# Another weight sequence for a list-scheduled attention block

## The chip, the cores and the metric

The kernel runs on one core of a Trainium2 chip. The metric is device time in microseconds for one call, the median of three runs. Five engines work side by side and meet through semaphores: TensorE (PE) multiplies, with its weight loads (PEld) recorded apart; VectorE (DVE), ScalarE (ACT) and GpSimd (POOL) work on tiles; SyncE (SP) mostly issues transfers.

## The reference

One residual layer of an encoder, S = 512 tokens, D = 1024, all in float32. A single input projection feeds two token mixers. A is multi-head latent attention: low-rank latents are normalised and projected up to 8 heads, with a rotary key that all heads share. B is sparse attention: a light indexer scores the keys, each query keeps 256 of them, with a relative bias. Each branch is gated, projected and weighted, the sum goes through an output projection and a last norm.

```python
h = rmsnorm(x, norm_g)
cq, ckv, kr, za, qb, kb, vb, zb, qi, ki, wi, ga, gb = split(h @ w_in)
# A: q = rms(cq) @ w_uq, [k_nope, v] = rms(ckv) @ w_ukv, rope on q_pe and kr
logits = q_nope . k_nope + q_pe . k_pe            # chunk-causal mask, softmax, @ v
# B: score = sum_h relu(qi_h . ki) * wi_h ; idx = top_k(score, 256)
logits = qb . kb[idx] * scale + rel_bias[bucket]  # softmax, @ vb[idx]
y = sigmoid(ga)*((A*silu(za)) @ w_o_a) + sigmoid(gb)*((B*silu(zb)) @ w_o_b)
out = rmsnorm(x + y @ w_out, final_g)
```

(shortened; splits, biases and reshapes are left out)

## The kernel before, in words

Every float32 operand is split into a high part and a remainder in a rounded format, and each product is made of three TensorE matmuls: high by high, high by low, low by high (`mm3`, which calls `mm`). Tokens stand in four tiles of 128, the 1024 input channels in eight. x is loaded and normalised, turned, and multiplied by the latent and indexer columns first. Then the weights are gone through tile by tile, each 128 x 1024 or less.

What sets the order of all work is a scheduler that runs while the kernel is built, the class `Flow`. Each piece of work is a thread, a generator that yields steps (an instruction group, with the engines that could do it and a duration), requests for a buffer, or conditions. `Flow.run` holds a clock for each engine and one for the transfers, asks for each waiting step when it could start (`start`: engine free, inputs written, readers of the output done), adds to that a safety time for PE and SP (`settled`, 1 to 2 us behind another engine's result), and emits the step with the lowest key. What it emits is fixed: at run time each engine works its list in order and waits at semaphores.

The weight tiles go through three threads, in the order of a list of jobs. `fetcher` has SP load each tile into one of four raw buffers, `splitter` splits it (a cast on ACT, the remainder on DVE or POOL), `multiplier` runs the job's matmuls. The string `QUEUE` gives the jobs' sequence by two-letter names: ga and gb are gate tiles, za and zb tiles of the SiLU paths, pe the rotary part of q, ma0 to ma3 two heads each of the up-projection of A, va its values, sb q and k of B, and ou the output projection's loads; names in capitals are pairs of tiles that `seven` multiplies with seven products in place of eight.

Eight PSUM banks ps0 to ps7 carry all products. A step that writes a bank waits for the readers of what stood in it. Around the change these names matter: `latraw`, the raw latents, scaled by rstd and by sm and then turned by PE (`turn`) into ps banks, from which ACT and DVE make `lat` with two instructions; L932 (L928 after), the relative bias as a product of a one-hot tile, copied by ACT; L883 (L879 after), one head's indexer scores for one token tile, then a ReLU on ACT in the bank, then a multiply-add into `mask` on DVE; and `mla_job`, where ACT and DVE split a head pair into `th` and `op`, SP moves halves of them to other partitions and adds the rotary rows (`qpe`, `kpeh`, `kpel`), and L1582 to L1584 (L1570 to L1572 after) form the logits. Four loads, jobs 7 to 10 of the list, are held back by `hold` until SP has issued 2 or 6 further transfers (`PASSED`), and one remainder of B's values is emitted late, at the next `add` of `seven` (`passed_by`).

Of the kernel before, what the change touches and what calls it, by code (L numbers as in the profile page):

```python
# [43 lines left out]
class Buf:  # L44


    def __init__(self, tile, name):
        self.tile, self.name, self.w, self.r, self.written = tile, name, 0.0, 0.0, False
        self.by, self.reads = None, {}
# [90 lines left out]
class Flow:  # L140
# [57 lines left out]
    def run(self, stop=None):  # L198
        while self.threads:
# [64 lines left out]
DRAW = 53  # L264
# [6 lines left out]
def tile_block(ctx: ExitStack, tc: tile.TileContext, a: dict, out: bass.AP, bias_dram: bass.AP):  # L271
# [25 lines left out]
    ps_bufs = set(id(b) for b in PS.free)  # L297

# [113 lines left out]

    def mm(ps, pairs, start, stop, more=False):
# [6 lines left out]
        t = len(pairs) * (0.0133 + pairs[0][1].n / 2400)  # L420
# [9 lines left out]
    def turn(parts):  # L430
# [6 lines left out]
        return pe(0.107 * len(parts), [d for d, _ in parts], [s for _, s in parts] + [ident.all], emit, len(parts))  # L437

    held = []

    def hold(n, emit):

        return lambda: held.append([n, emit])

    def passed():
        for x in list(held):
            x[0] -= 1
            if not x[0]:
                held.remove(x)
                x[1]()  # L450

    def dma(dst, src):

        d, s = (v.ap if isinstance(v, View) else v for v in (dst, src))
        n = 4
        for x in (dst.ap if isinstance(dst, View) else src.ap).shape:
            n *= x
        return Step([("SP", n / 360000.0, lambda: (nc.sync.dma_start(d, s), passed()))], bufs(dst), bufs(src))
# [25 lines left out]
    def pool_dma_out(dst, src):  # L484
        step = Step([("POOL", 1.03, lambda: nc.gpsimd.dma_start(dst, src.ap))], [], bufs(src))
# [391 lines left out]
    def scores(i):  # L877
        n = P * (i + 1)
        work = mask[i]  # L879
        for h in range(NH):  # L880
            yield Until(lambda: h in qs and ks)
            ps = yield bank("lg")
            yield pe(0.005 + n / 2400, [ps.all], [qs[h].all, ks[0].all], lambda: nc.tensor.matmul(  # L883
# [265 lines left out]
    def values2():  # L1149
# [69 lines left out]
        def take(half, out):  # L1219
            v = yield Get(VV)  # L1220
            for u in range(2):
# [4 lines left out]
                step = lo_part(lo, src, hi)  # L1226
                if half == 1 and u == 0:

                    step.options = [(e, t, lambda emit=emit: passed_by.append(emit)) for e, t, emit in step.options]
                yield step  # L1230
# [141 lines left out]
    qpe, operands = {}, {}  # L1372
# [34 lines left out]
    def mla_job(j):  # L1407
        lat_users[0] += 1

        def take(ps, kind):  # L1410
# [31 lines left out]
            if j == 3 and not kind:  # L1442
                put(*qpe[0], *qpe[1])
# [110 lines left out]
    def mla_head(h):  # L1554
# [18 lines left out]
        for i in ORDER:  # L1573
# [12 lines left out]
            yield pe(3 * (0.0133 + nn / 2400), [ps.all], [qh.all, ql.all, kh.all, kl.all], emit, 3)  # L1586
# [497 lines left out]
SUMS_AT = ("a", 5)  # L2084
# [83 lines left out]
```

## Time and profile before

| what | value |
|---|---|
| time, median of 3 runs | 423.46 us (423.2 to 423.58) |
| span of the profiled execution | 421.2 us |
| PE busy | 413.7 us (98%), 2314 matmuls |
| DVE, ACT, POOL busy | 372.8, 265.6, 125.2 us |
| mean granted TensorE clock | 0.995 |
| share of PE in the chain of waits | 96% |
| HBM read, written | 50.49 MB, 4.21 MB |

The span runs from the first to the last instruction of one profiled execution; the timed runs are 2.26 us longer, at the median. In rows of the timeline the first number is the start in us, the second the time that the group took; `x6` counts its instructions, and a bracket tells how long the engine stood idle before it and for whom. PE rows overlap, since matmuls are pipelined: the distance from one start to the next is what a matmul costs. Buffer numbers are left out there: `ps` is any bank.

### The profile page before, as it was taken

The numbers are of one execution on the slowest core, as the hardware profiler recorded it, in microseconds if no ns is written. First come the engines' busy times: TensorE is split into PE (matmuls) and PEld (weight loads), VectorE is DVE, ScalarE is ACT, GpSimd is POOL, SyncE is SP. The second block draws the span as 40 slices with busy tenths as digits, with TensorE's granted clock in tenths as the row PEclk, the third lists the DMA queues.
The fourth block names the chain that finished last, engine by engine and source line by source line (L and its number), as shares of the span: only waits on it lengthen the run. The fifth ranks groups of instructions, "written<-read, shape, count | busy, mean of one in ns | idle before, by whom it ended". The sixth has DMA issues, their size and how long they took to land.

```text
span 421.2 us, 7078 instructions
## 1 busy us (share of the span) xinstructions
PE 413.7 (98%) x2314; PEld 364.3 (86%) x2314; DVE 372.8 (89%) x797; ACT 265.6 (63%) x596; POOL 125.2 (30%) x139
## 2 busy tenths in 40 slices
PE   8999999999999999999999999999999999999994
PEld 7999878888888888888999988998998888888883
DVE  4879889569999999999999999979799768999995
ACT  5877778586754748625578677694597444336624
POOL 0047768543464669400012000200100000120652
PEclk9999999999999999999999999999999999999998
DMA  7992135665266441444652347144542887248305
GB/s 258 382 337 77 48 94 191 172 206 127 75 156 184 89 151 51 119 146 149 151 163 75 110 142 188 56 166 129 153 138 68 292 296 242 102 148 305 123 1 199
DMA packets 30645, 65.89 MB, mean 156 GB/s; under 512 B 4776, under 2 KB 6200, under 8 KB 30608
## 3 DMA queue, kind: packets, MB, share of 16 engines
q1 hardware_dynamic: 28256, 61.66, 47.4%
q10 hardware_dynamic: 1584, 2.62, 1.7%
q0 software_dynamic: 768, 1.15, 0.9%
q8 instruction: 18, 0.29, 0.3%
q14 instruction: 19, 0.16, 0.1%
HBM read 50.49 MB, written 4.21 MB: 130 GB/s over the span
## 4 chain that ended last, share of the span: by engine, by line
PE 96%; DVE 1%; DMA 1%; issue 0%; POOL 0%; ACT 0%; POOLq 0%; SPq 0%; ACTq 0%
PE ps L418 86%; PE ps L435 5%; PE ps L1583 1%; PE ps L1584 1%; PE ps L1582 1%; PE ps L883 1%; DMA normg<-norm_g 1%; DVE s_xr L357 1%; POOL sm L396 0%; DVE s_rg L357 0%; DVE s_rg L376 0%; ACT s_rg L329 0%; POOLq L2164 0%; ACT s_xg L329 0%; PE ps L932 0%
## 5 line engine op out<-in xcount | busy, mean ns | idle before, releaser
L418 PE MATMUL ps<-s_h,s_w 128*128 128x512 f32 (+1 forms) x732 | 169.9, 379 | 0.0
L418 PEld LDWEIGHTS ps<-s_h,s_w 128*128 128x128 f32 x732 | 128.3, 189 | 22.0
L320 ACT CAST s_w<-raw 128x512 fp32r<-128x512 f32 (+3 forms) x124 | 71.8, 593 | 18.8 <-DMA raw<-w_o 9.3
L348 POOL TENSOR_TENSOR s_w<-raw,s_w 128x512 fp32r<-128x512 f32 (+2 forms) x39 | 48.5, 1255 | 48.1 <-ACT s_w L320 44.2
L346 DVE TENSOR_TENSOR s_w<-raw,s_w 128x512 fp32r<-128x512 f32 (+2 forms) x85 | 55.7, 668 | 4.7 <-ACT s_w L320 3.7
L418 PE MATMUL ps<-s_ys,s_w 128*128 128x512 f32 x192 | 43.8, 389 | 0.0
L418 PEld LDWEIGHTS ps<-s_ys,s_w 128*128 128x128 f32 x192 | 36.0, 188 | 7.5
L329 ACT ACTIVATE s_p<-s_p,sm 128x128 f32<-128x128 f32 (+3 forms) x62 | 32.7, 550 | 5.0 <-DVE sm L1662 4.3
L418 PE MATMUL ps<-s_wo,s_mg 128*128 128x512 f32 (+1 forms) x156 | 33.2, 373 | 0.0
L418 PE MATMUL ps<-s_w,s_xg 128*128 128x328 f32 (+1 forms) x192 | 32.5, 323 | 0.0
L418 PEld LDWEIGHTS ps<-s_wo,s_mg 128*128 128x128 f32 x156 | 27.6, 188 | 5.2
L418 PEld LDWEIGHTS ps<-s_w,s_xg 128*128 128x128 f32 x192 | 31.4, 188 | 0.0
L346 DVE TENSOR_TENSOR s_ph<-ps,s_ph 128x384 fp32r<-128x384 f32 (+1 forms) x48 | 27.6, 593 | 1.0 <-ACT s_ph L320 0.7
L320 ACT CAST s_ph<-ps 128x384 fp32r<-128x384 f32 (+1 forms) x48 | 23.4, 515 | 6.4 <-PE ps L435 5.0
L329 ACT ACTIVATE s_p<-ps,sm 128x128 f32<-128x128 f32 (+3 forms) x32 | 16.8, 527 | 15.7 <-DVE sm L1565 15.6
L348 POOL TENSOR_TENSOR s_p<-s_bias,mask 128x128 f32<-128x128 f32 (+2 forms) x5 | 4.2, 854 | 74.0 <-DMA s_bias<-bias_scratch 39.6
L905 DVE MAX8 sm<-mask 128x8 f32<-128x384 f32 (+2 forms) x48 | 25.7, 549 | 0.2
L906 DVE MATCH_REPLACE8 mask<-sm,mask 128x384 f32<-128x384 f32 (+2 forms) x48 | 25.9, 541 | 0.0
L418 PE MATMUL ps<-s_ph,vv 128*128 128x512 f32 (+3 forms) x128 | 25.1, 318 | 0.0
L435 PE MATMUL ps<-ident,s_p 128*128 128x128 f32 x160 | 23.1, 273 | 0.0
L418 PEld LDWEIGHTS ps<-s_ph,vv 128*128 128x128 f32 x128 | 21.0, 188 | 2.4
L348 POOL TENSOR_TENSOR s_wo<-raw,s_wo 128x512 fp32r<-128x512 f32 x3 | 13.2, 4420 | 28.3 <-ACT s_wo L320 28.3
(194 smaller groups left out, 769.6 us busy)
## 6 DMA issues: line engine op xcount, KB each, us to landing
raw<-w_out SPq DMA_DIRECT2D x18, 512.0 KB, 3.3
s_op<-s_op SPq DMA_DIRECT2D x36, 128.0 KB, 2.3
raw<-w_ga SPq DMA_DIRECT2D x8, 512.0 KB
raw<-w_gb SPq DMA_DIRECT2D x8, 512.0 KB
raw<-w_o SPq DMA_DIRECT2D x16, 256.0 KB, 4.2
s_xn<-x SPq DMA_DIRECT2D x8, 256.0 KB, 4.8
bias_scratch<-s_sig ACTq DMA_DIRECT2D x8, 256.0 KB, 3.0
raw<-w_za SPq DMA_DIRECT2D x4, 512.0 KB, 4.7
```

The costliest lines, as they stand in the source:

```text
L320: nc.scalar.copy(dst.ap, src.ap)
L329: nc.scalar.activation(dst.ap, src.ap, func, **kw)
L346: opts.append(("DVE", 0.07 + 0.00104 * x.n, lambda: nc.vector.tensor_tensor(dst.ap, x.ap, y.ap, op=op)))
L348: opts.append(("POOL", 0.15 + 0.0021 * x.n, lambda: nc.gpsimd.tensor_tensor(dst.ap, x.ap, y.ap, op=op)))
L357: lambda: nc.vector.scalar_tensor_tensor(dst.ap, x.ap, sc(s), y.ap, op0=op0, op1=op1))],
L418: nc.tensor.matmul(ps.ap, l.ap, r.ap, start=start and i == 0, stop=stop and i == len(pairs) - 1, skip_group_check=more)
L435: nc.tensor.transpose(d.ap, s.ap, ident.tile)
L883: yield pe(0.005 + n / 2400, [ps.all], [qs[h].all, ks[0].all], lambda: nc.tensor.matmul(ps.tile[:, :n], qs[h].tile[:96, TOK[i]], ks[0].til ...
L905: yield Step([("DVE", t, lambda: nc.vector.max(m8.tile, work.tile))], [m8], [work])
L906: yield Step([("DVE", t, lambda: nc.vector.match_replace(work.tile, m8.tile, work.tile, MARK))], [work], [m8])
L1582: nc.tensor.matmul(o, q0[0:100], k0[0:100], start=True, stop=False)
L1583: nc.tensor.matmul(o, q0[0:96], k1[0:96], start=False, stop=False)
```

## The change

The scheduler's model gets other clocks. A step that reads a PSUM bank now also waits, in the model, for other engines' reads of it. A transfer takes SP 0.46 or 0.55 us to issue (0.05 before, beside a queue clock of its own), its first packet comes 1.0 or 1.2 us later, its duration is scaled by 0.935 (1.8 from buffer to buffer), and it lands 1.4 us behind that. A matmul counts at least 0.1155 us, a transpose 0.109. The seed of the threads' random nudges is another. The string QUEUE is another sequence. The held loads (`PASSED`, `hold`, `passed`) and the late remainder (`passed_by`) are gone, and the four tiles of rotary queries are given back once all four head pairs have used them, in whatever order, no more at pair 3.

```diff
@@ Flow.start
+            if b.bank:
+                for e, r in b.reads.items():
+                    if e != eng:
+                        s = max(s, r + self.lat(e, eng))
@@ Flow.run
-                self.free["SP"] = s + 0.05
-                self.hw = max(self.hw, s) + (0.65 if step.ins and step.outs else 0.475)
-                self.dma = max(self.dma, self.hw + 0.65)
-
-                self.dma += dur * (SLOW if self.dma < 7.3 else 1.0)
-                end = self.dma + (2.2 if step.ins and step.outs else 1.0) + step.late
+                both = step.ins and step.outs
+                self.free["SP"] = s + (0.55 if both else 0.46)
+                first = s + (1.2 if both else 1.0)
+                self.dma = max(self.dma, first) + dur * (1.8 if both else 0.935) * (SLOW if self.dma < 7.3 else 1.0)
+                end = max(self.dma, first + dur * (1.8 if both else 1.47)) + LANDING + step.late
...
-DRAW = 53
+DRAW = 46
...
+    def span(columns):
+
+        return max(0.0133 + columns / 2400, 0.1155)
...
-        t = len(pairs) * (0.0133 + pairs[0][1].n / 2400)
+        t = len(pairs) * span(pairs[0][1].n)
...
-        return Step([("SP", n / 360000.0, lambda: (nc.sync.dma_start(d, s), passed()))], bufs(dst), bufs(src))
+        return Step([("SP", n / 360000.0, lambda: nc.sync.dma_start(d, s))], bufs(dst), bufs(src))
...
-            if n in PASSED:
-
-                step.options = [("SP", step.options[0][1], hold(PASSED[n], step.options[0][2]))]
             yield step
...
-            step = tt(dst, part(ps), y, ALU.add)
-            return step.then(lambda: [passed_by.pop()() for _ in list(passed_by)])
+            return tt(dst, part(ps), y, ALU.add)
...
-            if j == 3 and not kind:
-                put(*qpe[0], *qpe[1])
+            if not kind:
+                qpe_users.append(j)
+                if len(qpe_users) == 4:
+                    put(*qpe[0], *qpe[1])
...
-QUEUE = 'ga0 ga1 pe ma0 va0 ga2 za0 ma1 va1 ga3 za1 ma2 ga4 za2 ma3 ga5 za3 sb0 zb0 ga6 ga7 sb1 VB GB0 GB1 sb2 zb1 GB2 GB3 sb3 zb2 GB4 GB5 ou zb3 gb6 ou gb7 ou'
+QUEUE = 'ga0 va0 ga4 ga7 za0 pe ga1 ma0 ma2 ga2 za2 ma1 gb3 va1 ma3 zb0 sb1 sb0 zb1 ga5 ga6 za1 VB za3 ou sb2 sb3 gb7 ga3 GB0 GB1 zb3 ou GB2 GB6 GB4 GB5 ou zb2'
+LANDING = 1.4
-PASSED = {7: 2, 8: 2, 9: 2, 10: 6}
```

What this does to the lists shows at two places. The first is PE's list at the relative bias and the second set of latents, some 300 rows in. Before, one one-hot product (into ps4, later one into ps3) stands apart, with other matmuls behind it:

```order
L932 MATMUL ps4_96<-s61_oh109_599,rbs_126 8x320
L883 MATMUL ps7_99<-s30_qs139_740,s21_qs102_570 128x256
L883 MATMUL ps5_97<-s30_qs139_740,s21_qs102_570 128x384
L418 MATMUL ps1_93<-s27_h121_653,s72_w130_704 128x512
...
L435 MATMUL ps6_98<-ident_100,s5_latraw132_717 128x128
...
L932 MATMUL ps3_95<-s71_oh129_694,rbs_126 8x320
L435 MATMUL ps4_96<-ident_100,s5_latraw132_717 128x128
...
L418 MATMUL ps0_92<-s25_h111_607,s18_w140_745 128x512
...
L435 MATMUL ps3_95<-ident_100,s5_latraw132_717 128x128
```

After, both products follow each other, and scores take their banks eight transposes later; ps4 is turned into twice (four rows each, one shown):

```order
L879 MATMUL ps7_99<-s16_qs137_733,s61_qs110_592 128x256
L879 MATMUL ps3_95<-s16_qs137_733,s61_qs110_592 128x384
L928 MATMUL ps5_97<-s7_oh121_652,rbs_126 8x320
L928 MATMUL ps0_92<-s34_oh127_697,rbs_126 8x320
L444 MATMUL ps4_96<-ident_100,s71_latraw130_711 128x128
...
L444 MATMUL ps1_93<-ident_100,s71_latraw130_711 128x128
...
L879 MATMUL ps5_97<-s16_qs137_733,s61_qs110_592 128x512
L879 MATMUL ps0_92<-s16_qs137_733,s18_qs126_687 128x256
L427 MATMUL ps6_98<-s37_h128_703,s3_w133_719 128x512
...
L444 MATMUL ps4_96<-ident_100,s71_latraw130_711 128x128
...
L427 MATMUL ps7_99<-s21_w139_737,s0_lat135_727 128x256
```

The work between a product and the next use of its bank has become less. ACT's list of the new kernel, which serves these banks, has there:

```order
L334 ACTIVATE s2_latraw132_717<-ps3_95,rstd_124 128x384
L334 ACTIVATE junk_113,sm3_79<-ps4_96,rstd_124 128x384
L334 ACTIVATE s17_latraw138_735<-ps4_96,rstd_124 128x384
...
L325 CAST s37_h128_703<-s10_tmp122_658 128x512
L325 CAST s21_w139_737<-raw0_66 128x512
L334 ACTIVATE ps7_99<-ps7_99 128x256
L334 ACTIVATE ps3_95<-ps3_95 128x384
L325 COPY s22_tmp142_748<-ps5_97 8x320
L325 COPY s23_tmp143_749<-ps0_92 8x320
L334 ACTIVATE s32_lat149_815<-ps4_96,glat_102 128x512
```

The four scalings into `latraw` are new on ACT; they were DVE's before.

The second place is SP's list where the operands of the second pair of heads are moved. Before (rows 94 on):

```order
L458 DMA qhi0_72<-s40_th267_1572 64x512
L458 DMA s46_op278_1619<-s4_op269_1574 64x512
L458 DMA qhi0_72<-s2_qpe187_1004 32x512
L458 DMA raw0_66<-w_kb 128x1024
L458 DMA s55_op275_1608<-s29_op271_1588 64x512
L458 DMA s64_op282_1639<-s37_op273_1590 64x512
L458 DMA s4_op269_1574<-s34_qpe188_1005 32x512
L458 DMA qhi1_73<-s2_qpe187_1004 32x512
L458 DMA s46_op278_1619<-s34_qpe188_1005 32x512
L458 DMA s29_op271_1588<-kpeh_107 36x512
L458 DMA s37_op273_1590<-kpel_108 32x512
```

After:

```order
L454 DMA raw3_69<-w_kb 128x1024
L454 DMA qhi1_73<-s41_th249_1448 64x512
L454 DMA qhi0_72<-s41_th249_1448 64x512
L454 DMA s59_op258_1496<-s14_op251_1450 64x512
L454 DMA qhi0_72<-s50_qpe198_1161 32x512
L454 DMA s29_op255_1481<-s31_op253_1464 64x512
L454 DMA s30_op259_1511<-s11_op254_1465 64x512
L454 DMA raw0_66<-w_qb 128x1024
L454 DMA s14_op251_1450<-s43_qpe199_1162 32x512
L454 DMA qhi1_73<-s50_qpe198_1161 32x512
L454 DMA s31_op253_1464<-kpeh_107 36x512
L454 DMA s11_op254_1465<-kpel_108 32x512
```

The load of w_kb stands ahead of the moves now, and one of w_qb among them; on PE, 59 rows (28 of 512 columns, 20 transposes, 11 shorter matmuls) lie between the last matmul of the operand that becomes s31_op253 and the first product that reads it, where 68 lay before, 46 of them of 512 columns.

More of the change, by code (lines that the diff above doesn't have):

```diff
@@ L48, in __init__ @@
         self.tile, self.name, self.w, self.r, self.written = tile, name, 0.0, 0.0, False
-        self.by, self.reads = None, {}
+        self.by, self.reads, self.bank = None, {}, False
     def __getitem__(self, idx):
@@ L250, in run @@
                 elif step.moves:
-                    self.dma = max(self.dma, end + 1.0) + step.moves
-                    end = self.dma + 1.0
+                    self.dma = max(self.dma, end + 1.0) + step.moves * 0.935
+                    end = max(self.dma, end + 1.0 + step.moves * 1.47) + LANDING
             for b in step.ins:
@@ L297, in tile_block @@
     ps_bufs = set(id(b) for b in PS.free)
+    for b in PS.free:
+        b.bank = True
     def in_ps(v):
@@ L435, in emit @@
                 nc.tensor.transpose(d.ap, s.ap, ident.tile)
[L437 to L450, printed above, removed]
+        return pe(0.109 * len(parts), [d for d, _ in parts], [s for _, s in parts] + [ident.all], emit, len(parts))
     def dma(dst, src):
@@ L457, in dma @@
             n *= x
-        return Step([("SP", n / 360000.0, lambda: (nc.sync.dma_start(d, s), passed()))], bufs(dst), bufs(src))
+        return Step([("SP", n / 360000.0, lambda: nc.sync.dma_start(d, s))], bufs(dst), bufs(src))
     def pool_dma(dst, src):
         s = src.ap if isinstance(src, View) else src
-        step = Step([("POOL", 1.03, lambda: nc.gpsimd.dma_start(dst.ap, s))], bufs(dst), bufs(src))
+        step = Step([("POOL", 0.55, lambda: nc.gpsimd.dma_start(dst.ap, s))], bufs(dst), bufs(src))
         step.moves = 4.0 * dst.n * dst.ap.shape[0] / 360000
@@ L484, in pool_dma_out @@
     def pool_dma_out(dst, src):
-        step = Step([("POOL", 1.03, lambda: nc.gpsimd.dma_start(dst, src.ap))], [], bufs(src))
+        step = Step([("POOL", 0.55, lambda: nc.gpsimd.dma_start(dst, src.ap))], [], bufs(src))
         step.moves = 4.0 * src.n * src.ap.shape[0] / 360000
@@ L882, in scores @@
             ps = yield bank("lg")
-            yield pe(0.005 + n / 2400, [ps.all], [qs[h].all, ks[0].all], lambda: nc.tensor.matmul(
+            yield pe(span(n), [ps.all], [qs[h].all, ks[0].all], lambda: nc.tensor.matmul(
                 ps.tile[:, :n], qs[h].tile[:96, TOK[i]], ks[0].tile[:96, :n], start=True, stop=True))
@@ L954, in fetcher @@
         yield is_done("loads")
-        for n, job in enumerate(jobs):
+        for job in jobs:
             raw = yield Get(RAW)
@@ L1098, in proj2 @@
         Job(a[second[0]][second[1]], [512, 512], body, prep=prep)
-    passed_by = []
     def seven(times, part, c11, c21, c12, c22, end):
@@ L1225, in take @@
                 yield act(hi, src)
[L1226 to L1230, printed above, removed]
+                yield lo_part(lo, src, hi)
                 put(out[u])
@@ L1371, in tile_block @@
     SC_A = (NOPE + RD) ** -0.5
-    qpe, operands = {}, {}
+    qpe, operands, qpe_users = {}, {}, []
     lat_users = [0]
@@ L1584, in emit @@
                 nc.tensor.matmul(o, q1[0:96], k0[0:96], start=False, stop=True)
-            yield pe(3 * (0.0133 + nn / 2400), [ps.all], [qh.all, ql.all, kh.all, kl.all], emit, 3)
+            yield pe(3 * span(nn), [ps.all], [qh.all, ql.all, kh.all, kl.all], emit, 3)
             spawn(soft(i, ps), prio)
```

2 lines of the change are left out of this document (1 added, 1 removed).

## The prediction

> **What bounds the kernel now.** I read the busy table and the chain of waits of the page first, then what TensorE waits for, then stretches of time, and last single instructions. The page:
>
> ```profile
> PE 413.7 (98%) x2314; PEld 364.3 (86%) x2314; DVE 372.8 (89%) x797; ACT 265.6 (63%) x596; POOL 125.2 (30%) x139
> PE 96%; DVE 1%; DMA 1%; issue 0%; POOL 0%; ACT 0%; POOLq 0%; SPq 0%; ACTq 0%
> PE ps L418 86%; PE ps L435 5%; PE ps L1583 1%; PE ps L1584 1%; PE ps L1582 1%; PE ps L883 1%; DMA normg<-norm_g 1%; DVE s_xr L357 1%; POOL sm L396 0%; DVE s_rg L357 0%; DVE s_rg L376 0%; ACT s_rg L329 0%; POOLq L2164 0%; ACT s_xg L329 0%; PE ps L932 0%
> ```
>
> TensorE (PE) is the chain that ended last for 96% of the span. The list of PE's waits has one row, and the busy time by stretches of 20 or 40 us shows no gap between 10 and 410 us:
>
> ```profile
> PE ps L541 <- DVE neghalf L492: 1.1, 1, 1.1
> 0.00:10.00 10.00, 8.82 (x50) 7.57 (x51) 4.91 (x13) 5.61 (x12) 0.55 (x6) 1.00 0.79 251
> 40.00:60.00 20.00, 20.00 (x107) 16.85 (x106) 16.89 (x26) 14.53 (x32) 12.72 (x17) 1.00 0.23 61
> 90.00:130.00 40.00, 40.00 (x226) 34.75 (x225) 37.54 (x88) 26.66 (x64) 21.02 (x29) 1.00 0.48 123
> 280.00:320.00 40.00, 40.00 (x245) 35.77 (x244) 34.57 (x76) 28.42 (x65) 1.76 (x1) 1.00 0.47 142
> 360.00:380.00 20.00, 20.00 (x90) 16.57 (x89) 20.00 (x39) 8.22 (x15) 4.25 (x3) 1.00 0.35 121
> 410.00:422.00 12.00, 4.91 (x33) 4.30 (x31) 6.35 (x19) 5.26 (x13) 2.86 (x4) 0.80 0.46 175
> ```
>
> The columns are busy time and count of PE, its weight loads (PEld), VectorE (DVE), ScalarE (ACT), GpSimd (POOL), then PE's granted clock, DMA share and GB/s. What the reader is to see: PE stands idle 1.2 us in the first ten, and 6.3 us between 410 and the span's end at 421.2, and nowhere else that shows, at clock 1.00. A 512-column matmul costs 20.00 / 90 = 0.222 us. So an order can win only at the two ends, and each microsecond for which PE is made to wait in the middle is a microsecond on the end.
>
> **The change part by part.** The order lists hold the same 2329 rows on PE and 240 on SP before and after; ACT goes from 521 to 529, DVE from 746 to 735, POOL from 144 to 145. PE's rows up to the end of the latent projection (44.8 us) and the last hundred are the same in kind and order, and so are SP's first 32 loads. So the two ends, where PE idles, do not move: gain 0. PE's sum of work stays at 413.7: 0 (if the mean distance of its 2314 matmuls moved by 1 ns, that would be 2.3 us; this is a rival below). The new clocks, DRAW and QUEUE act through the order alone, and no instruction gets slower by them.
>
> *Weight loads, and the removed hold of loads 7 to 10.* The sequence of tiles is new, so each load is issued elsewhere on SP. What covers it is the distance between a load and its use:
>
> ```profile
> 118.72 0.33 SPq L458 DMA_DIRECT2D raw<-w_za  x1
> 138.86 0.61 ACT L320 CAST s_w<-raw 128x512 fp32r<-128x512 f32 x1
> raw<-w_za SPq DMA_DIRECT2D x4, 512.0 KB, 4.7
> ```
>
> This load lands 4.7 us after its issue and its first half is cast 20 us after it. The new lists keep four raw buffers and about as much work between load and use, so I take 0; without that cover one late tile costs up to the 4.7 us. The four moved qpe releases free slots later by at most one head's operands: 0, for the same reason. Work moved between engines (eight latent scalings from DVE to ACT, some onto POOL) costs 0 in sum, as ACT is busy 63%; where it stands in a queue ahead of something PE needs, it counts in place A.
>
> *Place A, after about 51 us.* Here the new order lets PE take PSUM banks back right behind their readers: the two one-hot products (L928) go to ps5 and ps0, and eight transposes later two score products (L879) want ps5 and ps0 again; the latents' transposes use ps4 twice with three matmuls between. Before, the same kinds of instructions stood like this:
>
> ```profile
> 50.99 0.31 PE L932 MATMUL ps<-s_oh,rbs 64*8 64x320 f32 x1
> 51.23 0.56 PE L883 MATMUL ps<-s_qs,s_qs 96*128 96x256 f32 x2
> 51.34 0.42 ACT L320 COPY s_tmp<-ps 8x320 f32<-8x320 f32 x1 [0.37 <-PE ps L932]
> 51.63 0.85 PE L418 MATMUL ps<-s_h,s_w 128*128 128x512 f32 x3
> 53.09 0.66 PE L435 MATMUL ps<-ident,s_latraw 128*128 128x128 f32 x4
> 53.50 3.00 PE L418 MATMUL ps<-s_h,s_w 128*128 128x512 f32 x12
> 55.34 0.69 ACT L329 ACTIVATE s_lat<-ps,glat 128x512 fp32r<-128x512 f32 x1
> 55.92 0.40 ACT L320 COPY s_tmp<-ps 8x320 f32<-8x320 f32 x1
> 56.06 0.75 DVE L357 SCALAR_TENSOR_TENSOR s_lat<-ps,glat,s_lat 128x512 fp32r<-128x512 f32 x1
> 56.37 0.42 PEld L435 LDWEIGHTS ps<-ident,s_latraw 128*128 128x128 f32 x4 [0.29 <-ACT s_tmp L320]
> L329 ACT ACTIVATE ps<-ps 128x256 f32<-128x256 f32 x8 | 3.0, 379 | 1.4 <-PE ps L883 1.4
> L329 ACT ACTIVATE junk<-ps,rstd 128x384 f32<-128x384 f32 x4 | 2.3, 581 | 0.1
> L329 ACT ACTIVATE ps<-ps 128x384 f32<-128x384 f32 x8 | 3.8, 471 | 0.2 <-PE ps L883 0.2
> L365 DVE TENSOR_SCALAR mask<-ps,widx x3: 484/607/741, 59.1 to 60.9; 128x256 f32<-128x256 f32 x1, 128x384 f32<-128x384 f32 x1, 128x512 f32<-128x512 f32 x1
> ```
>
> The row at 56.37 says that the cover was thin already: the weight load waited for the copy that ended at 56.32, and PE went on 0.05 us behind it. In the old order 3.3 us of PE work (four transposes and 12 matmuls, 53.09 to 56.37) lay between the product and that reuse; in the new one it is eight transposes. I reckon both chains from the start of the first 256-column score, t = 0.
> - PE: the two scores 0.40 (51.63 − 51.23), two one-hot products 0.24 each (51.23 − 50.99), eight transposes at 0.41 for four (53.50 − 53.09): it wants ps5 at 1.70.
> - ACT starts 0.35 behind a product (51.34 − 50.99), then two ReLUs (0.38 + 0.47), then the copy of ps5 (0.42): 1.62, with 0.05 to PE 1.67. No stall. The copy of ps0 ends at 2.04, so PE may go at 2.09 and was there at 1.70 + 0.22 = 1.92: 0.17.
> - ACT's s_lat from ps4 takes 0.69 more (2.73), DVE's half, 0.03 behind it, 0.75 (3.51), PE may turn ps4 at 3.56. It has a 256-column score (0.12) and three matmuls (0.67): 2.88. Stall 0.68.
> - Four transposes (0.41) bring PE to 3.97; it wants ps7, which DVE's first mask row (0.48) leaves at 3.51 + 0.48 + 0.05 = 4.04: 0.07.
>
> Sum 0.9, if ACT is free at t = 0.35. Ahead of it ACT now scales four latents itself, which DVE did before (of the shape of the junk row, four in 2.3 us), and casts one h tile more (0.6, as the cast quoted above). In the stretch 40 to 60 ACT idled 5.5 us, so most of this fits; ACT can be late by 0 to 0.9, and this adds fully, since the chain hangs on ACT. I take 0.3: place A 1.2, from 0.5 (all hand-overs at their shortest) to 2.0.
>
> *Place B, after about 120 us.* Operands of an MLA head are moved by SP: halves of s_op to other partitions, and then the rotary rows kpeh and kpel, which L1570 and L1571 (L1582 and L1583 before) read. Before, in SP's timeline and, last, the view of the tile s_op:
>
> ```profile
> 119.71 0.60 ACT L329 ACTIVATE s_op<-ps 128x512 fp32r<-128x512 f32 x1 [0.28 <-PE ps L418]
> 121.67 0.53 SPq L458 DMA_DIRECT2D raw<-w_kb  x1
> 122.30 1.10 SPq L458 DMA_DIRECT2D s_op<-s_op  x2
> 125.75 0.54 SPq L458 DMA_DIRECT2D s_op<-s_qpe  x1
> 128.91 0.54 SPq L458 DMA_DIRECT2D s_op<-kpel  x1
> 132.73 0.23 PE L1582 MATMUL ps<-s_op,qhi 100*128 100x128 f32 x1
> DMA to landing us min/median/max: 2.0/2.3/4.8
> ```
>
> From ACT's half to the landing of kpel it took 128.91 + 2.3 − 119.71 = 11.5 us, in which SP stood still from 123.40 to 125.75 behind a move's semaphore; PE came 13.0 us behind ACT, 1.5 to spare. In the new order PE has between the operand's last matmul and L1570 59 rows, 28 of 512 columns (6.2 us), 20 transposes (2.1) and 11 of 128 to 384 columns (0.1 to 0.17 each, 1.5): 9.8 us. If SP stands still again, the stall is 11.5 − 9.8 = 1.7; without the stop the chain takes 9.2 and there is none. The weight load that I take for the cause (w_kb at 121.67, w_kb too in the new list) now stands ahead of the chain, not in it, but another (w_qb, one issue of 0.53) stands in it. I take 0.2, from 0 to 1.7 (to 4.2, should kpel need the 4.8 of the longest move).
>
> [...]
>
> *Place C, 284 to 321 us.* The paired (Strassen) tiles take banks back behind reads of a quarter:
>
> ```profile
> L346 DVE TENSOR_TENSOR s_pair<-ps,s_pair 128x256 f32<-128x256 f32 x15 | 6.2, 415 | 0.3 <-PE ps L418 0.3
> ```
>
> Three 256-column matmuls (0.36) can hide most of one such row. Bounds: 0 to 0.5 for some five places; I take 0.1.
>
> **The sum** is 421.2 + 1.2 + 0.2 + 0.1 = 422.7 us of span. The runs' median is 423.46, 2.26 above the profiled span of 421.2; with that, 425.0.
>
> **The rivals.**
> *(1) The waits are shorter than reckoned: no change.* If ACT is on time, and hand-overs at A cost nothing (0.5), and SP's stop at B is gone (0), the sum is 423.46 + 0.5 = 424.0. For it: before, banks came free 0.05 us ahead of PE with no wait. Against: the DVE half of s_lat behind ACT's on ps4 is alone 1.4 us against 0.8 of PE work.
> *(2) PE's matmuls come closer together: not slower.* Place: the whole of the middle. PEld is busy 86%, with 57 us free, so PE's 100% in the stretches may hide small gaps that another mix of long and short matmuls closes. Price 2.3 us per ns; it decides from 0.6 ns on, where it takes back the 1.5; at 0.9 ns the time is 425.0 − 2.1 = 422.9. Against: the stretch 360 to 380, all 512-column matmuls, has 0.222 with no weight load waiting, and the multiset is the same.
> [...]
> *(3) Longer waits: slower by more.* ACT 0.9 late at A (1.8), SP stopped at B (1.7), C at 0.5: 421.2 + 4.0 + 2.26 = 427.5. For it: at B the new order has 3.2 us less PE work than the old. Against: the load that stopped SP is issued earlier.
>
> **How the numbers follow.** The forecast (424.4 to 426.2, slower) has 0.50, (1) 0.26, (2) 0.08, (3) 0.16. What can be told from no change here is 0.2%, 0.85 us: 422.6 to 424.3. Faster: 0.06, three quarters of (2). Same: 0.24 of (1), 0.02 of (2) and 0.03 of the forecast's low edge: 0.29. Slower: 0.65. The range leaves out the tail of (2) and the far end of (3): 423.1 to 427.3.
>
> **What would show it.** In the new profile PE's list of waits must hold L879 and L444 on ACT and DVE near 51 to 55 us, 0.5 to 2 us in all, and the stretch 40 to 60 PE busy below 20.00; L1570 or L1571 on a DMA at 120 if B counts. If every stretch in the middle shows 20.00 of 20.00, my reckoning of A is wrong, and the time is 423.5. A wait for s_w on PE would show that the loads are not covered, which I exclude.

## The result, and the profile after

The changed kernel takes 427.0 us (median of four runs, 426.04 to 427.64) against 423.33 us for the kernel before in the same comparison: a ratio of 1.0078, with a 95% interval from 1.0065 to 1.009. It is slower by 3.7 us. The profiled execution has a span of 424.3 us, 3.1 above the 421.2 of before; at 426.04 us it is the shortest of the four (the others had spans of 424.8 to 425.9).

First the list of PE's waits, then stretches of the span, of the changed kernel. The columns of the stretches are those of the prediction.

```profile
PE ps L444 <- DVE s_lat L362: 1.1, 1, 1.1
PE ps L537 <- DVE neghalf L488: 1.1, 1, 1.1
PE ps L427 <- POOL s_w L353: 0.6, 1, 0.6
PE ps L427 <- DVE sm L1520: 0.5, 1, 0.5
PE ps L427 <- DVE s_pair L351: 0.2, 1, 0.2
...
0.00:10.00 10.00, 8.95 (x49) 7.57 (x50) 4.95 (x13) 5.68 (x12) 0.54 (x6) 1.00 0.78 245
40.00:60.00 20.00, 18.29 (x112) 16.17 (x111) 14.32 (x18) 16.26 (x37) 19.40 (x23) 1.00 0.30 87
90.00:130.00 40.00, 40.00 (x215) 34.56 (x214) 39.91 (x103) 23.33 (x59) 19.19 (x21) 1.00 0.67 184
200.00:220.00 20.00, 19.52 (x136) 18.16 (x135) 19.20 (x52) 12.56 (x32) 7.67 (x5) 1.00 0.14 41
280.00:320.00 40.00, 39.77 (x284) 37.31 (x283) 34.92 (x74) 29.75 (x67) 6.77 (x7) 1.00 0.33 97
360.00:380.00 20.00, 20.00 (x90) 16.57 (x89) 19.75 (x36) 7.55 (x14) 3.12 (x3) 1.00 0.35 114
```

Four waits are new, and all stand in the middle. The wait for neghalf at the start is that of before. PE idles in 40 to 60, in 200 to 220 and in 280 to 320; around 120 us (place B) it does not. The stretch 360 to 380 has the 90 matmuls that it had before, so their spacing is the same 0.222 us. POOL is busy for 19.40 of the 20 us from 40 to 60, where it was busy for 12.72.

What a wait costs is the distance from one start to the next, less the matmuls between, since their records overlap. In PE's timeline of the changed kernel:

```profile
53.08 0.84 PE L427 MATMUL ps<-s_h,s_w 128*128 128x512 f32 x3
54.99 0.66 PE L444 MATMUL ps<-ident,s_latraw 128*128 128x128 f32 x4 [1.07 <-DVE s_lat L362]
55.41 0.36 PE L427 MATMUL ps<-s_w,s_lat 128*128 128x256 f32 x1
56.41 0.86 PE L427 MATMUL ps<-s_w,s_lat 128*128 128x256 f32 x5 [0.64 <-POOL s_w L353]
...
214.77 2.32 PE L427 MATMUL ps<-s_w,s_h 128*128 128x256 f32 x18
217.58 1.67 PE L427 MATMUL ps<-s_w,s_hs 128*128 128x256 f32 x12 [0.48 <-DVE sm L1520]
...
316.95 1.60 PE L427 MATMUL ps<-s_h,s_w 128*128 128x256 f32 x12
318.79 1.43 PE L427 MATMUL ps<-s_hs,s_w 128*128 128x256 f32 x10 [0.23 <-DVE s_pair L351]
```

With 0.222 for 512 columns and 0.12 for 256 (three from 59.09 to 59.45 us in this kernel): 54.99 − 53.08 − 0.67 = 1.24; 56.41 − 55.41 − 0.12 = 0.88; 217.58 − 214.77 − 2.16 = 0.65; 318.79 − 316.95 − 1.44 = 0.40. The sum is 3.17, and the spans differ by 3.1. These four waits are the whole loss of the profiled execution.

Who was late at the first two? The other engines in the same microseconds:

```profile
52.62 0.67 ACT L334 ACTIVATE s_lat<-ps,glat 128x512 fp32r<-128x512 f32 x1
...
51.62 0.69 DVE L351 TENSOR_TENSOR s_h<-s_tmp,s_h 128x512 fp32r<-128x512 f32 x1
53.48 0.68 DVE L351 TENSOR_TENSOR s_tmp<-s_tmp,s_tmp 32x512 f32<-32x512 f32 x1 [1.17 <-POOL s_tmp L353]
54.19 0.75 DVE L362 SCALAR_TENSOR_TENSOR s_lat<-ps,glat,s_lat 128x512 fp32r<-128x512 f32 x1
...
49.47 2.26 POOL L384 TENSOR_SCALAR s_latraw<-s_latraw,sm 128x384 f32<-128x384 f32 x4
51.82 1.62 POOL L353 TENSOR_TENSOR s_tmp<-s_tmp,ropes 32x512 f32<-32x512 f32 x1
53.39 0.59 POOL L458 DMA_DIRECT2D s_qs<-s_th  x1
53.98 1.04 POOL L481 DMA_DIRECT2D bias_scratch<-s_tmp  x2
55.09 1.27 POOL L353 TENSOR_TENSOR s_w<-raw,s_w 128x512 fp32r<-128x512 f32 x1
```

ACT was on time: its half of s_lat ended at 53.29. DVE's half began only at 54.19: ahead of it in DVE's list stood the rotary key's sum (53.48), and before that DVE was idle for 1.17 us, until POOL had made one product (51.82 to 53.44). In the kernel before, DVE made that product itself, and POOL split s_w soon after the same four scalings:

```profile
49.28 2.27 POOL L379 TENSOR_SCALAR s_latraw<-s_latraw,sm 128x384 f32<-128x384 f32 x4
52.11 1.28 POOL L348 TENSOR_TENSOR s_w<-raw,s_w 128x512 fp32r<-128x512 f32 x1
...
52.61 1.33 DVE L346 TENSOR_TENSOR s_tmp<-s_tmp,ropes 32x512 f32<-32x512 f32 x1
```

Now POOL has the product too, and comes to it behind the four scalings. The second wait is POOL's as well: its half of the weight split, s_w, stands behind the product and three DMA issues, and starts 3 us later than before. So POOL's list, which holds work that the old order had given to DVE, stops PE twice.

At 217 and 318 us DVE reads a PSUM bank late that PE wants back. The profile names sm and s_pair there; DVE's and POOL's timelines give the order:

```profile
215.52 1.32 DVE L381 TENSOR_SCALAR s_p<-s_p,sm 128x512 f32<-128x512 f32 x1
216.75 0.68 DVE L351 TENSOR_TENSOR s_pair<-ps,s_pair 128x512 f32<-128x512 f32 x1
...
215.25 2.72 POOL L353 TENSOR_TENSOR raw<-raw,raw 128x512 f32<-128x512 f32 x2
...
317.61 0.69 DVE L351 TENSOR_TENSOR s_w<-raw,s_w 128x512 fp32r<-128x512 f32 x1 [0.35 <-ACT s_w L325]
318.22 0.42 DVE L351 TENSOR_TENSOR s_pair<-ps,s_pair 128x256 f32<-128x256 f32 x1
```

In both places the read of the bank (s_pair<-ps) stands one row behind a DVE instruction that nobody needed then: a scaling of softmax rows that took 1.32 us, and a weight split for which DVE first stood idle.

### The profile page after: what moved, and what is told of

Read it like the earlier page. It is cut to its first block, busy times and chain, and to the rows that moved or that the text cites. A ratio compares the mean times of both kernels' runs of the same rounds, so it can differ in the third digit from the quotient of the medians.

```text
span 424.3 us, 7136 instructions
## 1 busy us (share of the span) xinstructions
PE 414.5 (98%) x2314; PEld 364.9 (86%) x2314; DVE 368.9 (87%) x786; ACT 269.7 (64%) x604; POOL 127.1 (30%) x142
## 3 DMA queue, kind: packets, MB, share of 16 engines
q1 hardware_dynamic: 28256, 61.66, 47.6%
## 4 chain that ended last, share of the span: by engine, by line
PE 85%; DVE 5%; ACT 4%; POOL 2%; issue 2%; DMA 1%; POOLq 0%; DVEq 0%
PE ps L427 75%; PE ps L444 4%; PE ps L1571 1%; PE ps L1570 1%; PE ps L1572 1%; DVE s_w L351 1%; ACT junk L334 1%; PE ps L537 1%; PE ps L879 1%; DVE s_p L1650 1%; ACT s_latraw L334 1%; POOL sm L401 1%; DVE s_xr L362 1%; DMA s_raw<-onehot 1%; POOL s_latraw L384 0%
## 5 line engine op out<-in xcount | busy, mean ns | idle before, releaser
L353 POOL TENSOR_TENSOR s_w<-raw,s_w 128x512 fp32r<-128x512 f32 (+2 forms) x37 | 44.3, 1209 | 83.4 <-ACT s_w L325 68.5
L351 DVE TENSOR_TENSOR s_w<-raw,s_w 128x512 fp32r<-128x512 f32 (+2 forms) x87 | 57.3, 675 | 5.9 <-ACT s_w L325 4.9
L353 POOL TENSOR_TENSOR s_p<-s_bias,mask 128x256 f32<-128x256 f32 (+2 forms) x10 | 10.0, 1016 | 74.1 <-DVE s_p L351 24.1
L444 PEld LDWEIGHTS ps<-ident,s_p 128*128 128x128 f32 x160 | 18.9, 141 | 2.7
```

The costliest lines, as they stand in the source:

```text
L351: opts.append(("DVE", 0.07 + 0.00104 * x.n, lambda: nc.vector.tensor_tensor(dst.ap, x.ap, y.ap, op=op)))
L353: opts.append(("POOL", 0.15 + 0.0021 * x.n, lambda: nc.gpsimd.tensor_tensor(dst.ap, x.ap, y.ap, op=op)))
L444: nc.tensor.transpose(d.ap, s.ap, ident.tile)
```

## The experiments

All experiments but two take the changed kernel as it is, let the scheduler make the same plan with the same clocks, and change the emitted list alone. For this `Flow.run` counts its steps; a table says which step is emitted behind which later one, and a second table gives a step to another of the engines that it allows. Line numbers of the profile are higher by 8 or 10 in these kernels.

```diff
             t, (_, s, eng, dur, emit, _) = best
-            emit()
+            self.n += 1
+            emit = {e: m for e, _, m in t.req.options}.get(OTHER.get(self.n), emit)
+            if self.n in BEHIND:
+                self.behind.setdefault(BEHIND[self.n], []).append(emit)
+            else:
+                emit()
+            for e in self.behind.pop(self.n, ()):
+                e()
```

| kernel | time, us | ratio to before [95%] |
|---|---|---|
| changed kernel | 427.0 | 1.0078 [1.0065, 1.009] |
| k_order | 427.35 | 1.0089 [1.0074, 1.0104] |
| pool_order | 427.25 | 1.009 [1.0077, 1.0103] |
| both_a | 427.04 | 1.0087 [1.0073, 1.0102] |
| late_two | 425.69 | 1.0057 [1.0044, 1.0069] |
| pool_free | 426.19 | 1.0066 [1.0055, 1.0078] |
| free_and_late | 425.13 | 1.005 [1.0035, 1.0065] |
| old_queue | 431.37 | 1.0188 [1.016, 1.0215] |
| draw45 | 440.08 | 1.0394 [1.0364, 1.0424] |
| hold_both | 425.52 | 1.0048 [1.0035, 1.0062] |
| hold_free_late | 424.16 | 1.0018 [1.0009, 1.0026] |
| hold_all | 424.28 | 1.0022 [1.0014, 1.0031] |
| hold_alone | 427.25 | 1.0106 [1.0086, 1.0125] |

The kernel before measured 423.33 us beside the changed kernel, and 423.48, 423.26, 423.53 and 423.28 us beside the first four experiments, the next four, the next three and the last. An interval reaches some 0.5 us to each side, so the times alone do not tell apart two rows that differ by less than about 0.8 us; there the waits in the profiles have to decide.

**k_order.** The rotary key's sum on DVE, its cast on ACT and its remainder on POOL are emitted later, so that DVE does not stand in front of POOL's product.

```diff
+BEHIND = {346: 364, 356: 369, 366: 375}
```

> The changed kernel with its lists as they are, except that three instructions of the rotary key stand later: DVE's sum s_tmp (which waits for POOL) behind the next latents and masks, ACT's cast kpeh and POOL's kpel behind what followed them. DVE's half of s_lat then starts at about 53.3 in place of 54.2, and PE's first wait (1.1 us, for DVE s_lat, at 55.0) goes. Theory 'chain of POOL': the second wait (for s_w from POOL, over at 56.41) is set by POOL's own list and not by PE, so PE only waits longer there; time as the changed kernel's, 427.0, within 0.3. Rival 'each wait for itself': the first wait is won in full, 427.0 - 1.0 = 426.0.

Measured 427.35 us (427.12 to 427.97): no gain. In PE's timeline of this kernel:

```profile
53.69 0.84 PE L435 MATMUL ps<-s_h,s_w 128*128 128x512 f32 x3
54.75 0.66 PE L452 MATMUL ps<-ident,s_latraw 128*128 128x128 f32 x4 [0.21 <-DVE s_lat L370]
55.16 0.36 PE L435 MATMUL ps<-s_w,s_lat 128*128 128x256 f32 x1
57.00 1.31 PE L435 MATMUL ps<-s_w,s_lat 128*128 128x256 f32 x8 [1.47 <-POOL s_w L361]
```

The first stop shrank to 54.75 − 53.69 − 0.67 = 0.39, the second grew to 57.00 − 55.16 − 0.12 = 1.72. Together 2.11, as the 1.24 + 0.88 of the changed kernel. The two waits are not two costs: PE waits until POOL has done its list, and the first wait only took a part of it.

This profiled execution is the longest of the four, and its span of 426.2 us is 1.9 above the changed kernel's though these stops add up to the same. A part of that stands right behind the longer stop. In this row PE's granted clock is the third number from the right:

```profile
58.00:61.00 3.00, 3.00 (x16) 3.00 (x16) 1.33 (x4) 2.83 (x6) 2.84 (x3) 0.50 0.76 251
```

The clock is 0.50 there, where the changed kernel's profile has 1.00 from 56 to 62 us. The 20 matmuls of 256 columns from 57.00 on take 3.67 us to the next start, in place of 2.50 in the changed kernel: 1.17 us more. In this execution these 1.17 us, at the lower clock, came on top of the stop.

**pool_order.** POOL's s_w is emitted ahead of the three DMA issues.

```diff
+BEHIND = {340: 358, 349: 358, 354: 358}
```

> The changed kernel with one move: POOL makes the remainder s_w (which PE waits for at 56.4) ahead of its three DMA issues (0.6 + 1.0 us) in place of behind them. Both theories: POOL is done with s_w at about 54.8, so the second wait (0.9 us with the weight load) goes, the first (1.1 us at 55.0) stays: 427.0 - 0.9 = 426.1. If POOL's transfers matter to someone later, less is won.

Measured 427.25 us (426.72 to 427.98): no gain, against my expectation. The wait for s_w at 56.4 had gone, but PE stopped later, for 0.5 us at 60.19 for POOL's next s_w, and here:

```profile
70.30 0.53 PE L887 MATMUL ps<-s_qs,s_qs 96*128 96x256 f32 x2 [0.71 <-DMA s_qs<-s_th]
```

**both_a.** Both orders together.

```diff
+BEHIND = {346: 364, 356: 369, 366: 375, 340: 358, 349: 358, 354: 358}
```

> Both moves at place A together. Theory 'chain of POOL': now that s_w is there in time, the first wait is won as well: 427.0 - 1.9 = 425.1, more than the sum of the two alone (0 and 0.9). Rival 'each wait for itself': 427.0 - 1.9 = 425.1 as well, but as the sum of 1.0 and 0.9. If neither is right, and PE meets a new wait behind 57 us, less than 1 us is won.

Measured 427.04 us (426.27 to 428.45), another miss. Both waits near 55 us are down to 0.2 or gone, and the gain came back as one longer wait for the same transfer. Of PE's waits in this kernel:

```profile
PE ps L887 <- DMA s_qs<-s_th: 1.7, 1, 1.7
...
PE ps L452 <- DVE s_lat L370: 0.2, 1, 0.2
```

In its timeline, SP and then PE:

```profile
65.75 0.33 SPq L462 DMA_DIRECT2D raw<-w_uqkv  x1
66.18 1.15 SPq L462 DMA_DIRECT2D s_qs<-s_th  x2
...
70.32 0.53 PE L887 MATMUL ps<-s_qs,s_qs 96*128 96x256 f32 x2 [1.71 <-DMA s_qs<-s_th]
```

PE now came to the next indexer scores before their operands. What held the operands I took up again in the last four kernels.

**late_two.** At 217 and at 318 us, DVE's read of the bank is emitted ahead of the row that stood before it.

```diff
+BEHIND = {1342: 1344, 1936: 1939}
```

> The changed kernel with two rows of DVE's list exchanged at two places: at 217 us the scaling of s_p (1.3 us, beside a POOL instruction) behind the read of a PSUM bank (s_pair) that PE waits for, and at 318 us a weight remainder (which waits for ACT) behind another s_pair. If these waits (0.64 and 0.39 us between matmuls) are PE's loss at these places: 427.0 - 1.0 = 426.0. Rival, that the difference to the kernel before comes from place A alone and these are noise of one execution: 427.0.

Measured 425.69 us (425.25 to 426.78): 1.3 less, and neither wait is left in PE's list. The two stops cost 0.65 + 0.40 in the profile, so these two are shown by removal, one exchange of rows each.

**pool_free.** The order of k_order, and the rotary key's product and remainder given to DVE, which had them before.

```diff
+BEHIND = {346: 364, 356: 369, 366: 375}
+OTHER = {337: 'DVE', 366: 'DVE'}
```

> The changed kernel's lists with two POOL instructions on DVE (the rotary key's second product and kpel, 1.3 to 1.6 us of POOL each) and the three rows of the rotary key held back as in k_order. New theory 'POOL's list': between 40 and 70 us POOL's list (28.3 us busy of 30) is as tight as PE's, and sets the waits at 55.0 and 56.4 and, through the raw buffers and SP's s_qs moves behind them, the one at 70 that took the gain of both_a. With 2.9 us taken off POOL all three go: 427.0 - 1.9 = 425.1. Rival 'transfers': the wait at 70 is SP's alone (a move of s_qs behind a load, 4.1 us to landing); then the gain is lost again at 70 us, and the time is 426.5 to 427.0.

Measured 426.19 us (425.79 to 426.75), a gain of 0.8 where I expected 1.9. PE's waits:

```profile
PE ps L889 <- DMA s_qs<-s_th: 1.0, 1, 1.0
...
PE ps L454 <- DVE s_lat L372: 0.2, 1, 0.2
PE ps L437 <- POOL s_w L363: 0.2, 1, 0.2
```

The two waits near 55 us go from 1.1 and 0.6 to 0.2 and 0.2. POOL's list as their cause holds by this; the gain in time alone lies within the intervals. The third part of the theory, that POOL's list also sets the wait at 70 us, is not borne out: with two rows less on POOL that wait is still 1.0, and it took the rest of the expected gain.

**free_and_late.** pool_free and late_two together.

```diff
+BEHIND = {346: 364, 356: 369, 366: 375, 1342: 1344, 1936: 1939}
+OTHER = {337: 'DVE', 366: 'DVE'}
```

> pool_free and late_two together. If PE's five waits (55.0, 56.4, 70 us held off, 217, 318) are all that tells the changed kernel from the one before, the two gains add (1.9 and 1.3): 423.8, within 0.2% of the kernel before. If PE's work itself had become longer by the other order, 0.5 us or more above that remain; if it had become shorter, the time lies below the kernel before by as much.

Measured 425.13 us (425.05 to 426.74), span 423.3: the two gains add (0.8 and 1.3 of the 427.0 leave 424.9). The 423.8 that I expected was missed: PE still waits 1.0 for DMA s_qs.

**old_queue.** The new clocks and seed, without the held loads, with the sequence of weight tiles of before: is it the sequence that costs, or the plan that the clocks make?

```diff
-QUEUE = 'ga0 va0 ga4 ga7 za0 pe ga1 ma0 ma2 ...
+QUEUE = 'ga0 ga1 pe ma0 va0 ga2 za0 ma1 va1 ...
```

> The changed kernel (its model's clocks, its draw of nudges, no held loads) with the QUEUE string of before: the clocks alone. Theory 'the plan': what costs time is where a plan happens to pack a side engine's list, so any new plan is dearer than the tuned one by some waits of PE, 1 to 5 us, whatever part made it: 424.5 to 428. Rival 'the sequence': the new sequence of tiles alone is at fault, and the clocks are harmless: 423.5 within 0.5.

Measured 431.37 us (429.04 to 433.05), still slower than the changed kernel, and above what I gave to the theory. So the new sequence alone does not account for the loss: with the old one, the rest of the change plans worse yet. Its list of PE's waits has ten rows; beside neghalf, four of them are of 0.7 us and none is longer. The run does not tell what the new sequence would do with the old clocks; that was not measured.

**draw45.** The changed kernel with another seed of the random nudges.

```diff
-DRAW = 46
+DRAW = 45
```

> The changed kernel with one number changed, the seed of the threads' nudges (45 in place of 46), which are at most 0.01 us in the model. Theory 'the plan': another plan, another set of waits: anywhere from 425 to 432, and POOL's busy share between 40 and 70 us other than 28.3 of 30. Rival: sequence and clocks fix the time, and the seed moves it by less than 0.5: 426.5 to 427.5.

Measured 440.08 us (437.79 to 442.07), above what either theory or rival had given. One seed moves this kernel by 13 us; more than half of it is one wait, for a remainder of w_out near the end:

```profile
PE ps L427 <- DVE s_wo L351: 7.3, 1, 7.3
```

Behind this wait, which ends at 414.10, the granted clock is 0.50, too, from 414 to 417 us; its mean from 400 to 420 us is 0.83, and 1.00 from 380 to 400. POOL's list is as full from 40 to 70 us as in the changed kernel (28.10 us of 30, and 28.25 there), so the sign that I had named for the theory did not show. Since the change has a new seed as well, the experiments show which waits cost time in this plan, and leave open which part of the change (sequence, clocks or seed) put them there. The late remainder (`passed_by`) and the later release of the rotary queries were not tried alone.

**hold_both, hold_free_late, hold_all.** The wait for s_qs. In both_a the moves s_qs<-s_th stood in SP's list behind a load of 320 KB, raw<-w_uqkv. POOL had written s_th by 62.67 (61.66 + 1.01), but the load was issued at 65.75, after a wait for POOL to free a raw buffer (SP's four waits for POOL's s_w from 55 to 70 us make 15.0 us), and the moves behind it at 66.18. Counted along QUEUE from 0, this is load 7; the removed table `PASSED` had held load 7 back until 2 more transfers were issued, which here are the two moves. The edit does the same by hand, on three of the kernels above.

```diff
 hold_both (both_a and this):
+BEHIND = {346: 364, 356: 369, 366: 375, 340: 358, 349: 358, 354: 358, 429: 432}
 hold_free_late (free_and_late and this):
+BEHIND = {346: 364, 356: 369, 366: 375, 1342: 1344, 1936: 1939, 429: 432}
+OTHER = {337: 'DVE', 366: 'DVE'}
 hold_all (hold_free_late with the order of pool_order):
+BEHIND = {346: 364, 356: 369, 366: 375, 340: 358, 349: 358, 354: 358, 1342: 1344, 1936: 1939, 429: 432}
+OTHER = {337: 'DVE', 366: 'DVE'}
```

> both_a (the rotary key's three operations later on DVE, ACT and POOL, and POOL's s_w ahead of the three DMA issues) and one thing more: on SP, the load of 320 KB raw<-w_uqkv, which in both_a was issued at 65.75 us after a wait for a raw buffer that POOL frees, immediately ahead of the two moves s_qs<-s_th at 66.18, is issued behind these two moves. POOL had written s_th by 62.7, so the moves themselves waited only for the load. In both_a PE waited 1.7 us for them, until 70.32, 4.1 us after their issue. Theory 'the load ahead of the moves': the moves are issued some 3 us earlier, by 63.2, that wait goes to nothing, and the two orders of POOL show their gain at last: 427.0 - 1.7 = 425.3 us, span 423.8; no wait of PE for DMA s_qs. Rival 'the moves are late by themselves' (their sources, or what DMA has in flight then): the wait stays at 1 us or more, 426.5 to 427. A later load could cost too: the tile that it brings is split for a unit that PE begins after 72 us; then a new wait of PE for POOL's s_w between 72 and 80 takes the gain.

> free_and_late (rotary product and kpel moved to DVE, DVE's pairs of rows at 217 and 318 us exchanged) with the same load on SP issued behind the two moves s_qs<-s_th. free_and_late measured 425.13 us with span 423.3, and PE still waited 1.0 us for DMA s_qs until 68.98, the moves issued at 64.75 behind the load at 64.32. Theory 'the load ahead of the moves': the wait goes, span 422.2 to 422.3, 424.0 to 424.2 us: within 0.8 of the kernel before, the rest being the two waits of 0.2 at 54 and 55 us with their 0.36 and 0.42. Rival: no change, 425.1.

> hold_free_late and POOL's s_w ahead of its three DMA issues as in pool_order, all corrections together. It asks whether anything of the 3.7 us is left that is no wait of PE named so far. Theory 'all of it is waits': the stall of 0.42 for POOL's s_w at 55.2 goes as well, and at most the 0.36 for DVE's s_lat stays: span 421.6 to 421.9, 423.5 to 423.9 us, level with the kernel before (423.3). Rival 'something else in the new plan costs, such as the mean spacing of PE's matmuls': 424.5 or more though PE shows no wait above 0.2.

Measured: hold_both 425.52 us (425.26 to 426.26), 1.5 less than both_a. hold_free_late 424.16 us (423.94 to 425.57), 1.0 less than free_and_late, as the theory had it. SP's rows in hold_free_late, and PE's:

```profile
61.96 1.14 SPq L464 DMA_DIRECT2D s_qs<-s_th  x2
65.03 3.37 SPq L464 DMA_DIRECT2D raw<-w_uqkv  x2
...
66.52 2.22 PE L437 MATMUL ps<-s_h,s_w 128*128 128x512 f32 x9
68.58 0.46 PE L889 MATMUL ps<-s_qs,s_qs 96*128 96x256 f32 x2
```

The moves are issued at 61.96, where free_and_late had them at 64.75, and PE goes through without a stop. In hold_both the pattern repeats one unit later: the next four moves now follow two loads, and PE waits 0.5 at 73.25.

hold_all came out at 424.28 us (424.07 to 425.31), not lower than hold_free_late, though POOL's s_w was no longer waited for. Its rows on DVE, POOL and PE say why:

```profile
52.56 1.66 DVE L361 TENSOR_TENSOR s_h<-s_tmp,s_h 128x512 fp32r<-128x512 f32 x1
...
51.96 1.71 POOL L363 TENSOR_TENSOR s_w<-raw,s_w 128x512 fp32r<-128x512 f32 x1
...
54.27 0.73 PE L437 MATMUL ps<-s_h,s_w 128*128 128x512 f32 x2 [0.63 <-DVE s_h L361]
```

POOL's s_w, moved up, runs beside a DVE instruction of the same shape, which takes 1.66 us; in hold_free_late, where POOL issues DMAs at that time, it takes 0.69:

```profile
53.23 0.69 DVE L361 TENSOR_TENSOR s_h<-s_tmp,s_h 128x512 fp32r<-128x512 f32 x1
```

So neither theory of that run is right as written: the time is above the 423.9 that I gave to "all of it is waits", and the rival, a cost without a wait, is not shown either, since PE has a new wait of 0.63.

**hold_alone.** The changed kernel with the hold and nothing else.

```diff
+BEHIND = {429: 432}
```

> The changed kernel with nothing undone but this: on SP the load raw<-w_uqkv, at 64.41 us in the changed kernel, is issued behind the two moves s_qs<-s_th at 64.84 that follow it. It is the tile that the removed hold would by its number (7) have held behind 2 transfers. The prediction put the removal of the hold at 0. In the changed kernel PE comes to these operands at 69.05 without a wait, 4.2 us after the moves' issue, since it was stopped by 1.1 and 0.6 us before. Theory 'hidden behind place A': no change, 426.8 to 427.2 us, the waits at 55, 56, 217 and 318 us as they were; the hold is worth 1.0 to 1.2 us only where the stops at 55 and 56 are gone (425.13 to 424.16 and about 427.0 to 425.5 measured there). Rival 'the load costs by itself': 426.0 or less here too.

Measured 427.25 us (426.23 to 429.1): no gain; the list of PE's waits is the changed kernel's without its last row. The hold is worth 1.0 to 1.5 us where the stops near 55 us are gone, and nothing where they stand.

No kernel here beats the kernel before. hold_free_late comes to within 0.18% of it (0.09% to 0.26%), with six steps moved and two of the rotary key's steps given to DVE: of the 3.7 us, 0.6 are left, and each part that went was removed by an edit that names its wait. Two waits of 0.2 near 55 us are left in its profile, 0.39 and 0.43 by starts, about what is missing. At the first of them POOL holds nobody up any more; DVE's half of s_lat now waits for ACT's:

```profile
54.18 0.75 DVE L372 SCALAR_TENSOR_TENSOR s_lat<-ps,glat,s_lat 128x512 fp32r<-128x512 f32 x1 [0.25 <-ACT s_lat L344]
```

This is the chain by way of ACT that the prediction had reckoned for place A.

## Why the prediction was right, and where it was wrong

The direction was right: slower, for PE's waits in the middle of the span and nothing else. The size was 3.7 where I had 1.6, and 427.0 lies inside the range, near its upper end; that it does is in part luck, since the chain that I had reckoned for place A makes only 0.4 of the 3.17 us of stops. In the sum of spans: 422.7 reckoned, 424.3 found.

- **The floor** held. PE's stretches between the waits are 20.00 of 20.00, and the first ten and the end lose no more than before (from 410 us to the end of the span PE stands idle 14.3 − 8.01 = 6.3 us, as it did).
- **Place A** was mis-sized: 1.2 reckoned, 1.24 + 0.88 = 2.1 found. The place and the bank were right (DVE's half of s_lat, then the transposes into ps4), the engine was wrong. I let the chain hang on ACT and added 0.3 for its being late; ACT's s_lat ended at 53.29, 0.47 sooner than reckoned (2.73 behind the score at 51.03), and DVE's half came 0.9 later, not 0.03, because DVE stood in front of POOL. The chain that I had reckoned is worth 0.39, as k_order and hold_free_late show, where I had 0.68 and the 0.3. The copies of ps5 and ps0, for which I had 0 and 0.17, stopped nothing.
- **"Work moved between engines costs 0 in sum"** is the step that failed. I looked at the engine that got the most (ACT, busy 63%) and not at what the move did to POOL, whose busy time from 40 to 60 us went from 12.72 to 19.40. The prediction names work that went to POOL and gives it no price. k_order shows that POOL's list, and not DVE's one row in front of it, is what PE waits for, and in pool_free, with two rows taken off POOL, both waits fall to 0.2.
- **"A wait for s_w on PE would show that the loads are not covered, which I exclude"**: there is such a wait, of 0.88, at 56.41. The load was not late; the split of the tile was, on POOL. The distance from load to use, on which I rested, covers the load and not the split.
- **The removed hold at 0**: right for this kernel (hold_alone), and for the wrong reason. It is not covered by work; it hides behind the stops at place A, and costs 1.0 to 1.5 us as soon as these are mended.
- **Place B**: 0.2 reckoned, nothing found. SP's moves around 120 us came in time: from ACT's half at 114.24 to the landing of kpel (issued at 120.70, with 2.3 for the median move) it took 8.8 us, and PE's L1570 came at 124.22, 10.0 behind ACT; I had 9.2 without a stop of SP, and 9.8. With w_qb issued at 117.94 ahead of them, the moves landed 3.2 us after their issue at the longest.
- **Place C**: 0.1 reckoned, with bounds of 0 to 0.5. Found 0.40 at 318 us, within the bounds, and 0.65 at 217 us, which I had not seen: the same mechanism, a paired tile's bank that DVE reads late, ahead of the stretch that I looked at. Here what was late was a row that did not belong to the tile.
- **The rivals**: (1), no change, and (2), closer matmuls, did not come. (3), longer waits, came nearest with its 427.5, for other reasons: not ACT's lateness nor SP's stop at B.

The terms now read A 2.1, B 0, C and its like 1.05, which is 3.1 to 3.2. The other 0.4 to 0.6 us of the 3.7 lies between this profiled execution, the shortest of its four, and the median. The record does not show what fills it; a stretch at a lower clock, as in k_order, could (the mean granted clock of the longest of the four is 0.992, of the others 0.997 or more), and so could the stop at 29 us that is told at the end.

## What to carry to other kernels

When an order moves work from one engine to another, add up the list of the engine that receives it, instruction by instruction in the stretch, its DMA issues too; a busy share over the whole span (POOL had 30%) says nothing of it. A wait that was removed ahead of another only passed its time on (2.11 us of stops in k_order, 2.12 without its edit): mend the waits in the order in which PE meets them, and judge an edit by the sum of stops, not by the row that went. And a load put ahead of small moves in SP's list made the moves wait for the load's buffer, for 3.5 us in both_a (62.67 to 66.18); whether this showed depended on stops elsewhere, since taking the load out of the way won nothing in hold_alone, and 1.0 and 1.5 us in hold_free_late and hold_both, where the stops near 55 us were down to 0.2. Last, a new seed alone moved the time by 13 us here: with such a scheduler, a comparison of two plans tells little about the part of the change that made them differ.

## What the runs showed of the hardware that was not expected

At some places where DVE and POOL worked side by side, their instructions took longer than elsewhere. The scaling s_p<-s_p,sm of 128 x 512 took 1.32 us on DVE beside a POOL row (215.25, two instructions in 2.72 us); the list of groups has five of its shape in 3.2 us, so the other four took (3.2 − 1.3) / 4 = 0.48 each. In hold_all DVE's s_h took 1.66 in place of 0.69, and POOL's s_w 1.71 in place of the 1.27 that it has in the changed kernel at 55.09. The two overlap from 52.56 to 53.67, where POOL's row ends (51.96 + 1.71); DVE's went on to 54.22, 0.55 us longer. The rotary product took POOL 1.62 us beside the end of a DVE row; kpel, of the same shape, took it 1.28. In the changed kernel DVE's s_h<-s_tmp,s_h began at 39.74, ahead of three POOL rows of the same kind (40.00, 3.80 us in all), and took 4.62 us, where the same row at 51.62 took 0.69. It ended at 44.36, behind all three (43.80). No run here shows why.

The granted clock of PE was 0.50 behind two of its stops: from 58 to 61 us in k_order, behind 1.47 us of idle time (1.72 by starts), and from 414 to 417 us in draw45, behind 7.3 us. It stayed at 1.00 behind the 1.71 us of idle time at 70 us in both_a (the three 512-column matmuls from 70.69 took 0.70 to the next start, as in the changed kernel from 69.34), and from 56 to 62 us in the changed kernel. So the length of the stop alone does not decide it; what does was not tried.

The moves s_qs<-s_th reached PE 4.1 to 4.4 us after their issue where PE waited for them and a 320 KB load had gone out 0.43 us ahead (both_a, pool_order, pool_free, free_and_late). Whether the load ahead has a part in this time was not shown: the hold removes the load and SP's wait for its buffer together, and the issue 2.8 us earlier is enough for the gain.

Some executions of the same lists have one more stop of 0.3 to 0.8 us at 29 us, for ACT's s_rbc. PE's list there is that of the kernel before; ACT's is not: it copies s_rbc ahead of the last of a row of weight casts (behind it, before), and the cast in front of the copy waits for a load. The stop is 0.7 in both_a's profiled execution, 0.5 in hold_free_late's, and absent in free_and_late's and the changed kernel's. In hold_free_late ACT waited 1.20 us for the load of w_ql, until 28.48, and copied s_rbc at 28.90; in the changed kernel it waited 0.25, until 27.50, and copied it at 28.01. Why the load comes later in some executions was not tried.
